# Moving the gate projection of a hybrid attention and recurrence block out of the projection stream

## The chip, the cores and the metric

The kernel runs on one core of one Trainium2 chip. The metric is the device time of one execution in microseconds, the median of several runs. The engines of the core are PE (matrix products, with weight loads as PEld), DVE, ACT and POOL (elementwise work), and SP, which only issues transfers. Each engine works through its own queue in order; transfers are issued from the queues of SP and ACT.

## The reference

Two layers run one after the other. Each takes 2048 latent tokens and 256 context tokens of width 1024 and computes

```
h    = rmsnorm(x) * (1 + scale) + shift            # per layer, from the conditioning vector
p    = h @ w_in + b_in                              # columns for four mixers, and 1024 gate columns
ya   = differential attention (4 heads, 2 maps each, all keys)
yb   = HGRN2, a gated linear recurrence in both directions
yc   = sliding-window attention (window 128) plus the context, with sinks
yd   = mLSTM in both directions, times a sigmoid of p's output-gate columns
x    = x + gate * ((concat(ya, yb, yc, yd) * silu(p_gate)) @ w_out)
```

Layer 1 (the last one) writes no context tokens, and a final rmsnorm follows it. Large products are made in three half-precision passes (high*high, high*low, low*high parts) that add up in one accumulator; the recurrences use f32 products.

## The kernel before

Tokens come in tiles of 128: 16 latent tiles and 2 of context. Layer 0 works on 18 tiles in every mixer, layer 1 on 16 in its outputs. Both layers run through the same stages, in this order.

**h.** Rows of x are normalised, transposed on PE (`hps`, L417), scaled (`ht`, L419) and split into `hh` and `hl` (L421, L422), which stay in SBUF for all projections. The first projections follow (`first_blocks`).

**Differential attention.** The loop at L1170 runs over units of one head and one tile: 72 in layer 0, 64 in layer 1. A unit has two maps; for each, `diff_scores` makes two halves of scores on PE (`scr`), DVE finds their minima (L1048), and `diff_exp` on ACT takes the exponential straight from PSUM. Each of the two halves has one PSUM buffer. Between these steps `pump(ns)` feeds PE from a filler, the generator `other_blocks`, until so much PE time has been issued: FSTEP between the two halves of scores, FGAP twice per unit after them. PE's order is the order written in this loop. The filler is the remaining projections. It walks two lists side by side, `heavy` (mLSTM values and keys, sliding-window keys and queries, both HGRN gates) and `light` (HGRN values, sliding-window values, output gate, two query blocks, and at its end four blocks of `gate_silu`).

**Rest.** What the filler has left runs in `rest_stream`, beside the first tiles of sliding attention (`swa_stream`) and mLSTM (`mlstm_stream`). `weave` picks, by positions in units of tiles and by waits in PE time, which stream issues next; RPOS is how much filler goes with one tile. `room(i)` lets both streams run only two tiles ahead of the output until the filler is done.

**Final.** When the filler is done, `hp` (h), the weights and the staging tiles are freed, and `hgrn_stream` and `out_stream` join sliding attention and mLSTM. Outside the attention loop the order of instructions on each engine is made by a scheduler that works from program order and its own estimates, so work from later in the program may be issued early if its memory is free.

`gate_silu` (L910) makes, per block of 256 gate columns and pair of tiles (a gate set), 48 products of 256 columns, then z (two DVE steps), a sigmoid (three ACT steps) and a product on POOL, and writes 256 KB to DRAM (`dgt`). `out_stream` reads `dgt` back as `gtt` (512 KB a tile). The four mixers write into one SBUF tile `yt` per token tile, of which six exist, and only attention's quarter goes through DRAM (`dy`). `out_stream` multiplies `yt` by `gtt` on POOL, transposes it on PE (`ft`), splits it, and makes 48 products of 512 columns (`fx`, one PSUM buffer) with `w_out`, whose two parts are prepared at its start from eight loads of 512 KB (`braw`, one buffer).

## Time and profile before

| | us |
|---|---|
| median of 3 runs | 4201.5 (4193.78 to 4209.3) |
| the profiled execution's own time | 4220.02 |
| span in its profile | 4218.2 |
| PE, DVE, ACT, POOL busy | 3570.4, 2873.5, 2332.9, 2358.5 |
| mean granted TensorE clock | 0.901 of full |

Busy times count instructions only; waits, and the issue of transfers, are not busy time. A granted clock of 1.00 is 2.4 GHz, 0.50 is 1.2 GHz, and a stretch between has some of both. Products on PE overlap in the record, so the time that a row of products takes is best read from the start of one to the start of the next.

### The profile page before, as it was taken

The page shows a single profiled execution, that of the slowest core. Times are in us where ns is not written, and L with a number is a line of the kernel's source. Part 1 is how long each engine was busy: PE and PEld are TensorE (multiplying, and loading weights), DVE is VectorE, ACT ScalarE, POOL GpSimd, SP SyncE. Part 2 cuts the span into 40 slices and gives each one's busy share as a digit, 9 for nine tenths or more (in the row PEclk, how much of TensorE's full clock was granted, in tenths as well). Part 3 has the DMA queues.
Part 4 walks back from the last instruction along what each step waited for, and adds up shares of the span by engine and source line. Part 5 has one row for each costly group of instructions (what it writes and reads, how often), then busy time and mean ns, then how long its engine had stood idle before and what let it go on. Part 6 is the DMA issues. An engine that isn't in the chain of part 4 may idle for free.

```text
span 4218.2 us, 78854 instructions
## 1 busy us (share of the span) xinstructions
PE 3570.4 (85%) x30342; PEld 2395.7 (57%) x30342; DVE 2873.5 (68%) x4550; ACT 2332.9 (55%) x4679; POOL 2358.5 (56%) x1727
## 2 busy tenths in 40 slices
PE   6988878888769987989998888788876798789998
PEld 3656655444547675556656476544444575556665
DVE  5168888888885546556643499888899766556664
ACT  5245656666655545555653366666666664555663
POOL 4443555443445458778857545645344554677883
PEclk7999989999989986888999999999998999778998
DMA  5356866667666547467754467566776662646662
GB/s 205 100 138 151 189 131 165 135 150 157 127 142 165 134 133 174 143 167 170 184 152 142 121 133 158 126 147 150 151 161 132 155 163 84 166 124 161 169 169 76
DMA packets 1256960, 622.19 MB, mean 148 GB/s; under 512 B 913476, under 2 KB 1203848, under 8 KB 1256584
## 3 DMA queue, kind: packets, MB, share of 16 engines
q1 hardware_dynamic: 1154216, 490.64, 51.2%
q10 hardware_dynamic: 102368, 126.52, 8.9%
q8 instruction: 239, 3.92, 0.4%
q14 instruction: 137, 1.12, 0.1%
HBM read 291.76 MB, written 131.23 MB: 100 GB/s over the span
## 4 chain that ended last, share of the span: by engine, by line
PE 31%; DVE 18%; POOL 8%; issue 7%; DMA 7%; ACT 5%; SPq 1%; ACTq 0%; POOLq 0%; DVEq 0%
PE fx L94 7%; PE ptm L94 5%; PE pfm L94 5%; DVE sm L1048 4%; PE go L94 4%; PE mnum L94 3%; PE scr L94 2%; ACT p L105 2%; DVE p L111 2%; POOL E L108 2%; DMA swt<-ph 1%; POOL yt L108 1%; PE gA L94 1%; PE ss L94 1%; DVE sm L108 1%
## 5 line engine op out<-in xcount | busy, mean ns | idle before, releaser
L108 POOL TENSOR_TENSOR p<-p,p 128x1024 f16<-128x1024 f32 (+2 forms) x264 | 623.4, 2362 | 793.7 <-ACT p L1084 704.4
L94 PE MATMUL ptm<-wb,hh 128*128 128x256 f16 (+2 forms) x5024 | 834.6, 273 | 30.3 <-DVE tm L111 7.4
L105 ACT ACTIVATE p<-scr,sm 128x1024 f32<-128x1024 f32 (+2 forms) x528 | 628.2, 1194 | 416.4 <-DVE sm L1073 143.3
L1048 DVE TENSOR_REDUCE sm<-scr 128x1 f32<-128x1024 f32 (+2 forms) x528 | 698.9, 1326 | 218.0 <-PE scr L94 214.2
L94 PE MATMUL pfm<-hh,wb 128*128 128x512 f16 (+1 forms) x2592 | 809.0, 376 | 26.5 <-DVE gz L111 10.4
L94 PE MATMUL ptm<-wb,hl 128*128 128x256 f16 (+2 forms) x2512 | 671.9, 273 | 1.8 <-POOL hl L108 1.8
L94 PEld LDWEIGHTS <-wb 128*128 128x128 f16 x3888 | 378.8, 101 | 410.8 <-issue 81.1
L94 PE MATMUL scr<-Ks,Qs 128*128 128x512 f16 (+1 forms) x1296 | 364.5, 380 | 289.2 <-ACT p L105 284.1
L94 PEld LDWEIGHTS <-hh 128*128 128x128 f16 x5024 | 479.0, 100 | 131.3 <-issue 37.7
L94 PE MATMUL pfm<-hl,wb 128*128 128x512 f16 (+1 forms) x1296 | 488.1, 377 | 0.0
L111 DVE SCALAR_TENSOR_TENSOR p<-p,sm,p 128x1024 f32<-128x1024 f32 (+2 forms) x264 | 414.6, 1571 | 8.2
L94 PE MATMUL fx<-wo,mh 128*128 128x512 f16 x1088 | 371.8, 426 | 6.2 <-DVE xt L111 2.7
L94 PEld LDWEIGHTS <-Qs 128*128 128x128 f16 x1296 | 130.4, 102 | 429.9 <-issue 359.5
L1084 ACT CAST p<-p 128x1024 f16<-128x1024 f32 (+2 forms) x264 | 297.4, 1126 | 40.0 <-DVE p L111 35.3
L94 PEld LDWEIGHTS <-wt 128*128 128x128 f16 x4640 | 245.1, 103 | 71.7 <-DMA wt<-p 23.6
L94 PE MATMUL pv<-Vs,wt 128*128 128x128 f16 (+1 forms) x4640 | 259.6, 214 | 22.1 <-DMA wt<-p 14.6
L94 PEld LDWEIGHTS <-hl 128*128 128x128 f16 x2512 | 250.6, 100 | 36.1 <-POOL hl L108 3.3
L94 PE MATMUL fx<-wo,mlo 128*128 128x512 f16 x544 | 230.0, 423 | 6.1 <-DVE mlo L108 5.9
L108 POOL TENSOR_TENSOR E<-lk,cm 128x512 f32<-128x512 f32 (+1 forms) x136 | 205.3, 1510 | 41.2 <-DMA cm<-dhc 19.7
L108 POOL TENSOR_TENSOR ph<-swp,ph 128x640 f16<-128x640 f32 (+2 forms) x136 | 190.7, 1402 | 59.5 <-ACT ph L1326 45.1
L108 DVE TENSOR_TENSOR QQ<-hq,E 128x512 f32<-128x512 f32 x119 | 148.1, 1253 | 73.6 <-ACT E L105 35.9
L105 ACT ACTIVATE E<-E 128x1024 f32<-128x1024 f32 x136 | 143.0, 1052 | 99.5 <-POOL E L108 93.1
(298 smaller groups left out, 6853.7 us busy)
## 6 DMA issues: line engine op xcount, KB each, us to landing
wraw<-in_w_in_dram SPq DMA_DIRECT2D x60, 512.0 KB
dgt<-ga ACTq DMA_DIRECT2D x68, 256.0 KB
r1b<-dr SPq DMA_DIRECT2D x68, 256.0 KB
gtt<-dgt SPq DMA_DIRECT2D x34, 512.0 KB
mraw<-in_w_mod_dram SPq DMA_DIRECT2D x64, 256.0 KB
vi<-dhi SPq DMA_DIRECT2D x49, 256.0 KB
KSb<-dsk SPq DMA_DIRECT2D x56, 192.0 KB
Ks<-dka SPq DMA_DIRECT2D x64, 144.0 KB
```

Of the source, the lines that this page charges most:

```text
L94: PE.matmul(o, lhsT=lhsT, rhs=rhs, start=start, stop=stop)
L105: A.activation(out=o, in_=i, func=f, **kw)
L108: return e.tensor_tensor(out=o, in0=a, in1=b, op=op)
L111: V.scalar_tensor_tensor(out=o, in0=a, scalar=s, in1=b, op0=op0, op1=op1)
L1048: V.tensor_reduce(sm[:, m * 2 + j:m * 2 + j + 1], ps[:, :n], AX.X, ALU.min)
L1084: A.copy(wl[:, :n], p[:, :n])
```

## The change

The gate projection leaves the filler. `h` is written to DRAM (`dh`, 256 KB for each part and tile, 36 writes a layer from ACT's queue), and `hh` and `hl` are laid out by tile. A new `gate_stream` reads h back tile by tile in the final stage, holds all 1024 gate columns of the weights in SBUF, and makes 48 products of 512 columns per tile; its result `ga` stays in SBUF for `out_stream`. Sliding attention and mLSTM are no longer held back by the output: they run with the rest of the filler (RPOS 12000) until all of the three are done, and only then the final stage begins, with gate, output and HGRN. All mixers' outputs go through `dy`; `out_stream` loads whole rows of it one tile ahead. FSTEP goes from 1100 to 600 ns in both layers, FGAP from 2500 and 2360 to 2300. Smaller edits: the HGRN prefix sums of two tiles in one scan, four small copies (`dn`) less per mLSTM tile, two buffers for `fx`, `gz`, `braw`.

```
-YTB, GPB, FXB, EB = 6, 4, 1, 3
+YTB, GPB, GLAG, EB = 3, 3, 1.0, 3
-    [... 32192.0, 1100.0, 2500.0],      # layer 0: ..., FSTEP, FGAP
-    [... 22000.0, 1100.0, 2360.0],      # layer 1
+    [... 32192.0, 600.0, 2300.0],
+    [... 22000.0, 600.0, 2300.0],
-    [38826.0, 42669.0, 12000.0, ...],   # layer 0: RPOS, SW0, HG0, ...
-    [40000.0, 23476.0, 6974.0, ...],    # layer 1
+    [12000.0, 12000.0, 12000.0, ...],
+    [12000.0, 12000.0, 6974.0, ...],
...
+                for t in range(n):
+                    for j, a in enumerate((hh, hl)):
+                        DQ.dma_start(dh[g0 // P + t, :, j], a[g][:, t])
...
-                    for i in range(nt):
-                        ...
-                        V.tensor_tensor_scan(out=o_, data0=ones_c, data1=f_, ...)
+                    for i in range(0, n, 2 * P):
+                        o_ = cu[:, i:i + 2 * P]
+                        o_ = o_[:, ::-1] if d else o_
+                        V.tensor_tensor_scan(out=o_, data0=ones_z.rearrange("p t q -> p (t q)"), data1=o_, ...)
...
-            ] + [((C_GATE + cb * 256, 256), lambda w, cb=cb: gate_silu(w, cb)) for cb in range(4)]
+            ]
...
-                    yield i, 0.0 if i else SW0, room(i)
+                    yield i, 0.0 if i else SW0, None
...
-                    o1 = yt_of(i)[:, 512:768].rearrange("p (h d) -> p h d", d=64)
+                    o1 = sw.tile([P, 4, 64], F32, tag="so1", name="so1")
...
+                    SP.dma_start(dy[qt * P:(qt + 1) * P, 512:768], o1)
...
-                            V.tensor_copy(dn[:, 1, d * 2:d * 2 + 2], TM[:, 2, d, js[d] * 4 + pa_:js[d] * 4 + 4:2])
...
+                    SP.dma_start(dy[order[i] * P:(order[i] + 1) * P, 768:], hqf)
...
+                    SP.dma_start(dy[cols, 256:512].rearrange("(t p) c -> p t c", p=P),
+                                 O.rearrange("p (t h) d -> p t (h d)", t=2))
...
+            def gate_stream():
+                wg = [fo.tile([P, KC, D], F16, tag=f"wg{j}", name=f"wg{j}", bufs=1) for j in range(2)]
+                bg = fo.tile([P, D], F32, tag="bg", name="bgt", bufs=1)
+                SP.dma_start(bg, b_in[l, C_GATE:C_GATE + D].partition_broadcast(P))
+                for b in range(8):
+                    s_ = slice(b * P, (b + 1) * P)
+                    raw = fo.tile([P, KC, P], F32, tag="braw", name="graw")
+                    SP.dma_start(raw, w_in[l][:, C_GATE + b * P:C_GATE + (b + 1) * P].rearrange("(k p) n -> p k n", p=P))
+                    act(wg[0][:, :, s_], raw, AF.Copy, scale=WS)
+                    stt(wg[1][:, :, s_], raw, WS, wg[0][:, :, s_], ALU.mult, ALU.subtract)
+                    yield 0.2 * b, 0.0, None
+                def load(i):
+                    ht = fo.tile([P, 2, KC, P], F16, tag="ht", name="htile")
+                    SP.dma_start(ht, dh[order[i]])
+                    return ht
+                nxt = load(0)
+                for i in range(len(order)):
+                    at = i + GLAG
+                    yield at, 0.0, lambda: i < done["out"] + YTB
+                    ht = nxt
+                    if i + 1 < len(order):
+                        nxt = load(i + 1)
+                    ga = gts[i] = fo.tile([P, D], F32, tag="ga", name="ga", bufs=YTB)
+                    for j in range(2):
+                        s_ = slice(j * 512, (j + 1) * 512)
+                        ps = gps.tile([P, 512], F32, tag="gz", name="gzp")
+                        for k in range(KC):
+                            mm(ps, ht[:, 0, k], wg[0][:, k, s_], k == 0, False)
+                            mm(ps, ht[:, 0, k], wg[1][:, k, s_], False, False)
+                            mm(ps, ht[:, 1, k], wg[0][:, k, s_], False, k == KC - 1)
+                            yield at + 0.5 * j + 0.06 * k, 0.0, None
+                        z = fo.tile([P, 512], F32, tag="gz", name="gz")
+                        stt(z, ps, IWS, bg[:, s_], ALU.mult, ALU.add)
+                        V.tensor_scalar(z, z, ZLOW, None, ALU.max)
+                        sigmoid(ga[:, s_], z)
+                        tt(G, ga[:, s_], ga[:, s_], z, ALU.mult)
+                    done["gate"] = i + 1
...
+                    need = min(i + 1, len(order) - 1)
+                    yield at, 0.0, lambda: done["hg"] > need and done["gate"] > i
+                    yt, xt = nxt or out_load(i)
+                    nxt = out_load(need) if need > i else None
+                    ga = gts.pop(i)
...
-            join(rest_stream(), swa_stream(), mlstm_stream())
-            weave(lambda: done["rest"])
+            join(rest_stream(), swa_stream(), mlstm_stream())
+            weave()
             wst.close()
             hst.close()
...
-            join(out_stream(), hgrn_stream())
+            st4.close()
+            gps = st5.enter_context(tc.tile_pool(name=f"gpt{l}", bufs=2, reuse_waits="tile", space=PSUM))
...
+            join(gate_stream(), out_stream(), hgrn_stream())
             weave()
```

## Rows read from the trace of the kernel before

**Rows 1.** Stages: length; busy PE, PEld, DVE, ACT, POOL; clock, DMA share, GB/s.
```profile
237.00:1290.00 1053.00, 849.39 (x7434) 563.73 (x7432) 866.94 (x1293) 615.28 (x1012) 479.91 (x277) 0.93 0.66 149
1290.00:1555.00 265.00, 247.34 (x1994) 183.80 (x1993) 136.94 (x301) 133.78 (x287) 123.93 (x114) 0.95 0.50 136
1555.00:2216.00 661.00, 594.62 (x5358) 395.96 (x5355) 378.81 (x674) 375.13 (x1010) 495.90 (x412) 0.82 0.65 167
2216.00:2385.00 169.00, 153.24 (x995) 99.96 (x993) 54.20 (x73) 58.08 (x97) 114.62 (x96) 0.97 0.44 137
2385.00:3300.00 915.00, 725.85 (x6375) 478.51 (x6373) 810.98 (x1133) 573.90 (x893) 445.14 (x244) 0.95 0.66 143
3300.00:3632.00 332.00, 281.28 (x2269) 205.03 (x2270) 199.89 (x368) 177.75 (x354) 162.93 (x135) 0.91 0.50 131
3632.00:4218.00 586.00, 522.52 (x4736) 348.32 (x4736) 349.68 (x596) 316.23 (x871) 421.57 (x350) 0.82 0.58 147
```

**Rows 2.** Waits of PE and of DVE in layer 1's attention: us, times, longest.
```profile
PE scr L94 <- ACT p L105: 157.2, 109, 6.9
DVE sm L1048 <- PE scr L94: 81.5, 119, 4.7
```

**Rows 3.** Busy time in parts of the final and rest stages, columns as in Rows 1.
```profile
1559.00:1648.00 89.00, 65.50 (x594) 54.08 (x594) 61.07 (x94) 51.67 (x137) 68.66 (x58) 0.54 0.80 198
...
1700.00:2216.00 516.00, 483.52 (x4342) 311.68 (x4342) 294.10 (x537) 293.20 (x805) 385.75 (x325) 0.88 0.63 165
...
3500.00:3632.00 132.00, 103.74 (x788) 71.39 (x786) 68.93 (x121) 60.07 (x98) 52.27 (x42) 0.90 0.27 88
```

**Rows 4.** PE in order of time: start, length, product, count.
```profile
2058.30 0.33 PE L94 MATMUL spv<-SVc,swt 128*128 128x128 f16 x4
...
2058.72 0.59 PE L94 MATMUL fx<-wo,mh 128*128 128x512 f16 x2
...
2059.37 0.59 PE L94 MATMUL fx<-wo,mh 128*128 128x512 f16 x2
...
2060.60 0.39 PE L94 MATMUL ss<-KSc,QS 128*128 128x256 f16 x2
...
2061.36 0.46 PE L94 MATMUL gA<-QQ,E 64*64 64x64 f32 x14
...
2063.46 0.44 PE L94 MATMUL mnum<-v,r1b 128*128 128x65 f32 x2
...
2064.19 0.43 PE L94 MATMUL mnum<-v,r1b 128*128 128x65 f32 x2
```

**Rows 5.** Tiles fx, mnum, gA, go and ss, each in 1700 to 2216, busy by engine.
```profile
1700.00:2216.00 516.00, 221.92 (x781) 22.44 (x33) 0.88 0.63 165
1700.00:2216.00 516.00, 78.16 (x416) 63.06 (x416) 10.95 (x26) 4.36 (x26) 0.88 0.63 165
1700.00:2216.00 516.00, 54.29 (x1792) 42.17 (x1792) 33.06 (x84) 14.81 (x42) 0.88 0.63 165
1700.00:2216.00 516.00, 66.01 (x336) 56.64 (x336) 5.20 (x14) 0.88 0.63 165
1700.00:2216.00 516.00, 37.04 (x327) 34.54 (x43) 37.53 (x86) 0.88 0.63 165
```

**Rows 6.** Groups of instructions in layer 0's rest stage: busy us, mean ns.
```profile
L94 PE MATMUL pfm<-hh,wb 128*128 128x512 f16 (+1 forms) x224 | 67.8, 375 | 2.7 <-DVE gz L111 2.0 <-ACT kT L722 0.7
...
L108 POOL TENSOR_TENSOR ga<-ga,gz 128x512 f32<-128x512 f32 x24 | 30.7, 1279 | 51.6 <-ACT ga L105 45.3 <-DMA vi<-dhi 3.4 <-DVE gz L111 2.6
```

**Rows 7.** Groups of the gate on DVE in layer 1's attention stage.
```profile
L916 DVE TENSOR_SCALAR gz<-gz 128x512 f32<-128x512 f32 x8 | 6.7, 832 | 0.0
L111 DVE SCALAR_TENSOR_TENSOR gz<-ptm,bg 128x512 f32<-128x512 f32 x8 | 5.4, 679 | 0.0
```

**Rows 8.** Issue of the gate's writes on ACT's queue: ns min/median/max.
```profile
L919 ACTq DMA_DIRECT2D dgt<-ga x68: 366/377/1507, 1078.3 to 3628.9; - x68
```

**Rows 9.** Page of the profile, part 3: transfers by packet size, whole span.
```profile
DMA packets 1256960, 622.19 MB, mean 148 GB/s; under 512 B 913476, under 2 KB 1203848, under 8 KB 1256584
```

More of the change, by code (lines that the diff above doesn't have):

```diff
@@ L139, in sigmoid @@
         act(o, o, AF.Exp, scale=-1.0)
-    ones_c = const.tile([P, P], F32, tag="ones", name="ones_c")
-    V.memset(ones_c, 1.0)
+    ones_z = const.tile([P, 2, P], BF16, tag="ones", name="ones_z")
+    V.memset(ones_z, 1.0)
+    V.memset(ones_z[:, :, 0:1], 0.0)
     ws_t = const.tile([P, 1], F32, tag="ws", name="ws_t")
@@ L290 @@
         dog = dt_("dog", [T, 256])
-        dgt = dt_("dgt", [T, D])
+        dh = dt_("dh", [NT, P, 2, KC, P], F16)
         dy = dt_("dy", [T, D])
@@ L1198 @@
                     u1, u2, u3 = u, u1, u2
-        with ExitStack() as st4:
+        with ExitStack() as st5:
+            st4 = ExitStack()
             sw = st4.enter_context(tc.tile_pool(name=f"sw{l}", bufs=2, reuse_waits="tile", side="right"))
@@ L1204 @@
             gps = st4.enter_context(tc.tile_pool(name=f"gps{l}", bufs=1, reuse_waits="tile", space=PSUM, side="right"))
-            gps2 = hg = fo = None
+            hg = fo = None
             order = all_tiles(cq)
             ngrp = len(order) // 2
-            done = dict(sw=0, ml=0, hg=0, out=0, rest=0)
-            yts = {}
-            turn_ = [0]
+            done = dict(hg=0, gate=0, out=0)
             def bank(shape, name):
-                turn_[0] += 1
-                if gps2 and turn_[0] % GPB == 0:
-                    return gps2.tile(shape, F32, tag="gp", name=name)
-                return gps.tile(shape, F32, tag="gp", name=name, bufs=GPB - 1)
-            def yt_of(i):
-                if i not in yts:
-                    yts[i] = (ml if i % YTB < 2 else fo).tile([P, D], F32, tag="yt", name="yt",
-                                                              bufs=2 if i % YTB < 2 else YTB - 2)
-                    t = order[i]
-                    SP.dma_start(yts[i][:, 0:256], dy[t * P:(t + 1) * P, 0:256])
-                return yts[i]
-            def room(i):
-                return lambda: i < done["out"] + (YTB if done["rest"] else 2)
+                return gps.tile(shape, F32, tag="gp", name=name, bufs=GPB if fo is None else GPB + 1)
             def states_of(src, g, n, pool, tag):
@@ L1391, in mlstm_stream @@
                 for i in range(len(order)):
-                    yield i, 0.0 if i else SW0, room(i)
+                    yield i, 0.0 if i else SW0, None
                     js, qt_, kt_, v1, r1b, g0b, og = nxt
@@ L1574, in out_stream, with out_load @@
+                    yield 0.2 * b + 1.0, 0.0, None
+                def out_load(i):
+                    r_ = slice(order[i] * P, (order[i] + 1) * P)
+                    yt = fo.tile([P, D], F32, tag="yt", name="yt", bufs=YTB)
+                    xt = fo.tile([P, D], F32, tag="xt", name="xt", bufs=YTB)
+                    SP.dma_start(yt, dy[r_])
+                    SP.dma_start(xt, x_rows(order[i], 1))
+                    return yt, xt
+                nxt = None
                 for i, t in enumerate(order):
@@ L1584, in out_stream @@
-                    tt(G, yt[:, 0:512], yt[:, 0:512], gt_[:, 0:512], ALU.mult)
-                    tt(G, yt[:, 512:], yt[:, 512:], gt_[:, 512:], ALU.mult)
+                    need = min(i + 1, len(order) - 1)
[3 more added lines that the diff above has]
+                    ga = gts.pop(i)
+                    for j in range(2):
+                        s_ = slice(j * 512, (j + 1) * 512)
+                        tt(G, yt[:, s_], yt[:, s_], ga[:, s_], ALU.mult)
@@ L1632, in join, with weave @@
                 live.extend([*next(g), pe_ns[0], g] for g in gens)
-            def weave(until=None):
-                while live and not (until and until()):
+            def weave():
+                while live:
                     may = [e for e in live if e[2] is None or e[2]()]
```

104 lines of the change are left out of this document (39 added, 65 removed).

## The prediction

> **What bounds the kernel now.** I read the busy times by stage first, then the waits of the attention stage, then PE in order of time to get the true pace of its products.
>
> The stages of [rows 1] have different limits. In attention DVE is busy for 867 of 1053 us (82%) in layer 0 and for 811 of 915 us (89%) in layer 1, PE for 81% and 79%. The waits there form a ring [rows 2]: PE's scores wait for ACT's exponentials to empty their one PSUM buffer (157 us in layer 1), and DVE's minima wait for the scores (82 us). Whatever PE does between two halves of scores lengthens the ring, and DVE's own work is a floor under it.
>
> In the rest stage PE is busy 93% and 85%. In the final stage it is busy 90% and 89%, at a granted clock of 0.82. That stage has a bad start: from 1559 to 1648 the clock is 0.54 while PE is busy 65.5 of 89 us [rows 3], because the output's weights are not ready and only small f32 products run. From 1700 on PE is busy 94% at 0.88, and nothing else is near full: POOL 386 of 516 us.
>
> **A unit of work.** The sum is made in PE work at full clock. Three `fx` products take 0.65 us from start to start, 0.217 each [rows 4]; an output tile is 48 of them, 10.4 us, plus eight f32 transposes that I put at half of 0.217 each (an estimate): 11.3. The gate's 48 products of 512 columns are also 10.4; a gate set of 48 at 256 columns is 5.2, so the total gate work is the same before and after. Four `mnum` records take 0.73 us [rows 4], 32 of them a tile 5.8, with 0.9 for the mLSTM scores (same estimate) 6.7. Sliding attention takes 0.76 for scores and 0.42 for values per head [rows 4], 4.7 a tile. HGRN's `gA` and `go` are busy 120 us for 14 tiles (1792 records, 128 a tile) at clock 0.88 [rows 5]: 7.6 a tile.
>
> How much of this fits into a microsecond? From 1700 to 2216 the counts of [rows 5] are 16.3 output tiles, 14 HGRN tiles, 13 mLSTM tiles and 43 heads: 184 + 106 + 87 + 51 = 428 us of work in 516 us, 0.83. In layer 0's rest stage 24 gate sets (125), 14 HGRN projection blocks of 24 products (224 records and half as many with `hl`, 73) [rows 6], some 20 for their states and some 33 for the first tiles (both estimates) make 251 in 265 us, 0.95. The dense f16 share of the work is 0.37 in the one and 0.87 in the other; between them I interpolate.
>
> **h, +5 us a layer.** 36 writes are added to ACT's queue; one issue takes 377 ns [rows 8], 13.6 us a layer, and none is on PE. A write of `hl` waits for POOL's last difference of its group, and the next group's `hh` copies queue behind it on ACT, for which POOL waits in turn. The bounds are nothing (ACT is idle most of that stretch: 58 of 169 us busy in layer 1) and 14; I take 5. The writes of `dgt` and its reads, equal in bytes, go. The added writes and reads of `dy` on SP's queue stand behind transfers that wait for POOL and PE, but `out_stream` asks a tile ahead; the cover is a tile's 30 us, and without it a round trip would show at each tile.
>
> **Attention.** PE gets less filler: per unit 2 x 500 + 2 x 200 = 1.4 us in layer 0 (72 units, 101 us) and 2 x 500 + 2 x 60 = 1.12 us in layer 1 (64 units, 72 us). If the ring sets the pace, all of that comes back. If DVE does, only its work counts that leaves: 12 gate sets in layer 0 (36 less the 24 of [rows 6]) and 8 in layer 1, at 1.5 us [rows 7], so 18 / 0.82 = 22 and 12 / 0.89 = 14 us. The heavy list gets a larger share of what remains, so the rest of DVE's work stays. Both limits are near here, so I take the middle: -61 and -43.
>
> **Rest, now with all of sliding attention and mLSTM.** Filler left over: in layer 0 93 us (the 73 and 20 above) plus 101 - 12 x 5.2 = 39, so 132; in layer 1 93 + 72 - 8 x 5.2 = 123. RPOS gives 12 us of it to each tile, so it lasts for 11 and 10.3 tiles. Up to there the work is 132 + 11 x 11.4 = 257 and 240, dense share 0.51, pace 0.86: 298 and 278 us. The remaining 7 and 5.7 tiles have only the two mixers, and PE is no longer the limit. Their price has bounds of 13.7 (11.4 / 0.83) and 22 us a tile. The latter is their transfers: in the rest stage the DMA share is 0.50 [rows 1], with filler alone 0.27 [rows 3], so 60 us in layer 0 and 76 in layer 1 belong to some 3.5 tiles, 17 and 22 each. I take 17, since little else moves then: 119 and 97. The stage takes 417 and 375 us against 265 and 332: **+152 and +43**. The `dn` copies that go save DVE time that PE covers.
>
> **Final.** A tile is 11.3 + 10.4 + 7.6 = 29.3 us of work, 527 and 469 in all. The dense share rises to 0.74, the pace to 0.92: 573 and 510. POOL loses more than it gets, so PE stays the limit. At the start sixteen weight loads instead of eight must land and be split, but gate products need only the first eight; loads for this stage can start in the tail of the one before, where memory of h is free. I put 20 us on the start: 593 and 530 against 661 and 586, **-68 and -56**. The bounds are the pace of 0.83 (655 and 585) and 0.95 with no loss at the start (555 and 494).
>
> **Sum.** Layer 0: 5 - 61 + 152 - 68 = +28. Layer 1: 5 - 43 + 43 - 56 = -51. Together -23 us on the profiled execution's 4220, which is 18 above the median shown; on the median 4201.5 this gives 4179. Less than 0.5% (21 us) can't be told from no change here, so this sits at that edge: work is moved between stages that are nearly all full, and the gain is what the bad start of the old final stage cost, less the new tail.
>
> **Rivals.**
> *The third stage runs on transfers.* At 19.5 us of transfers a tile (the middle of 17 and 22), 0.27 per us of filler, and 8.4 MB of early weights at the 198 GB/s and share 0.80 of [rows 3] (34 us), layer 0 needs 351 + 36 + 34 = 421 and layer 1 379 us of all sixteen engines. At a share of 0.9, more than any stretch of [rows 1, 3] has, that is 468 and 421 instead of 417 and 375: +97, 4276. It decides from 18 us a tile on. For it: mixers' transposes are packed into half the time. Against it: 17 was the dearer tile, with context, in layer 0. Chance 0.17. The Trainium skill (DMA: Bandwidth & Descriptors, Specifications) says that full rate wants transfers of at least 512 bytes; the trace has 913,476 of 1,256,960 packets below that [rows 9], and no stage above 0.66 of its engines, so it shows no saturation yet.
>
> *DVE holds attention.* Then attention gives 22 and 14, not 61 and 43, while the filler still lands in the next stage: +68, 4247. DVE's 89% in layer 1 speaks for it, its 82 us of waiting for scores against it. It decides when DVE's busy share passes 0.92. Chance 0.17.
>
> *The ring alone holds attention.* All 173 us come back instead of 104: 4110. Layer 0's DVE has 186 us idle, which would allow it; layer 1 has only 104. Chance 0.15.
>
> *The dense final stage keeps the clock.* At pace 0.95 and with no loss at its start it takes 555 and 494: -74, 4105. For it: the clock is 0.95 to 0.97 in the dense stretches of [rows 1]; against it: HGRN's f32 products remain. Chance 0.16. The Trainium skill (TensorE: Matmul & The Clock Gate, HAM oscillation) says that PE falls to half clock when its work has gaps, so gate products that are always at hand would hold it up; the trace agrees as far as 0.54 at the starved start goes [rows 3].
>
> **Chances and range.** My own case has 0.35, about 4140 to 4220. Faster by over 0.5%: 0.16 + 0.15 + 0.16 of my case; slower: 0.17 + 0.17 less a little that ends near zero, and some of my case. That makes 0.47 faster, 0.19 same, 0.34 slower. The range takes in the four rivals with their own spread: 4075 to 4285.
>
> **What would show it.** Attention near 992 and 872 us, with DVE's share up and the wait of scores for ACT down. Sliding attention and mLSTM over some 420 and 375 us, slow only after the last HGRN projection, DMA share near 0.8 or below. A final stage of about 590 and 530 us whose clock is above 0.88 and has no long stretch at 0.5. I am wrong if the tail of the third stage costs over 20 us a tile, if attention shortens by less than its DVE work, or if the final stage waits on `dy` or on weights.

## The result and the profile after

The changed kernel takes 4457.2 us (median of 4, 4457.0 to 4459.9); the kernel before, run beside it, 4205.4 us (median of 4). The ratio is 1.0603 with a 95% interval of 1.0577 to 1.0629: 6% slower, where 4179 us had been forecast.

The stages of the profiled execution of the changed kernel, columns as in [rows 1]. The mixer stage (sliding attention and mLSTM) is split where mLSTM ends, the final stage near where the output's products begin.

```profile
0.00:246.00 246.00, 197.61 (x1201) 123.92 (x1202) 77.24 (x117) 82.12 (x157) 115.28 (x101) 0.93 0.55 184
246.00:1240.00 994.00, 754.02 (x6569) 482.98 (x6568) 860.45 (x1252) 584.66 (x963) 463.42 (x263) 0.92 0.69 148
1240.00:1605.00 365.00, 345.29 (x2229) 238.58 (x2226) 206.70 (x445) 205.73 (x642) 225.48 (x245) 0.83 0.76 185
1605.00:1715.00 110.00, 65.69 (x504) 49.01 (x503) 40.28 (x98) 49.84 (x106) 49.94 (x41) 0.50 0.69 136
1715.00:1800.00 85.00, 59.71 (x489) 35.71 (x489) 42.15 (x46) 40.84 (x70) 39.38 (x28) 0.67 0.66 200
1800.00:2325.00 525.00, 510.89 (x4127) 281.94 (x4123) 199.59 (x300) 254.39 (x531) 319.56 (x219) 0.91 0.33 109
2325.00:2500.00 175.00, 153.13 (x957) 100.14 (x958) 53.87 (x80) 53.82 (x93) 107.35 (x92) 0.90 0.60 201
2500.00:3420.00 920.00, 687.03 (x5909) 442.33 (x5908) 829.02 (x1126) 558.37 (x872) 438.39 (x245) 0.92 0.64 137
3420.00:3795.00 375.00, 340.50 (x2154) 238.18 (x2152) 226.61 (x442) 221.38 (x630) 241.90 (x234) 0.76 0.76 176
3795.00:3890.00 95.00, 56.27 (x478) 39.44 (x477) 44.64 (x103) 48.79 (x103) 54.58 (x45) 0.66 0.72 155
3890.00:3995.00 105.00, 67.83 (x661) 41.40 (x662) 70.61 (x70) 48.85 (x83) 57.21 (x38) 0.67 0.54 164
3995.00:4458.00 463.00, 446.83 (x3453) 244.46 (x3451) 181.62 (x260) 197.09 (x434) 227.26 (x166) 0.91 0.27 91
```

These windows, and those of [rows 1], do not cut the stages at the same event. Attention's last products are `pv`, and they start last at 1275.2 and 3329.4 in the kernel before, at 1243.4 and 3447.8 in the changed one (kernel before first, layer 0 and then layer 1):

```profile
L94 PE MATMUL pv<-Vs,wt x2336: 190/220/314, 285.2 to 1275.2; 128*128 128x128 f16 x195
L94 PE MATMUL pv<-Vs,wt x2304: 190/219/314, 2425.7 to 3329.4; 128*128 128x128 f16 x192
...
L94 PE MATMUL pv<-Vs,wt x2336: 190/220/314, 289.7 to 1243.4; 128*128 128x128 f16 x195
L94 PE MATMUL pv<-Vs,wt x2304: 192/220/314, 2549.1 to 3447.8; 128*128 128x128 f16 x192
```

[rows 1] ends attention 15 us behind and 29 us ahead of them, the windows above 3 and 28 us ahead. So from here on, wherever a stage's length is compared between kernels, its ends are events of the trace: attention goes from the first `scr` product to the last `pv`, the rest or mixer stage from there to HGRN's first `gA` product, the final stage from there to the next layer's first `scr` or to the end. Layer 1's h stage overlaps layer 0's final stage and is counted with it. Lengths and changes in us, layer 0 / layer 1:

| stage | before | after | change | forecast change | miss |
|---|---|---|---|---|---|
| h of layer 0 | 238 | 246 | +8 | +5 | +3 |
| attention | 1038 / 947 | 997 / 942 | -40 / -5 | -61 / -43 | +21 / +38 |
| rest, then mixers | 279 / 312 | 472 / 447 | +192 / +136 | +152 / +43 | +40 / +93 |
| final, with layer 1's h | 828 / 577 | 791 / 563 | -37 / -14 | -63 / -56 | +26 / +42 |

The misses sum to 263 us, of which 133 are in the mixer stage. The reader is to see three things in the windows. While filler runs beside the mixers, PE is busy 95% and 91%, at a clock of 0.83 and 0.76. Then PE is busy 60%, DVE and ACT under half, at 0.50 in layer 0, near the lower of the clock's two levels: 29 heads of sliding attention (87 records of `swp` on ACT, three a head) run alone there. And the new final stage starts with 85 and 105 us at 0.67; its first output product (`fx`) comes 76 and 94 us after the first `gA`, where I had put 20 on the start.

The waits of that lone stretch of layer 0, 1605 to 1715 (us, times, longest):

```profile
ACT swp L105 <- DVE ssm L1296: 54.7, 28, 2.7
DVE ssm L1295 <- PE ss L94: 46.5, 28, 3.1
PE spv L94 <- DMA swt<-ph: 28.8, 25, 3.0
```

and ACT's exponentials in its timeline:

```profile
1639.58 0.79 ACT L105 ACTIVATE swp<-ss,ssm 128x640 f32<-128x640 f32 x1 [2.14 <-DVE ssm L1296]
...
1643.18 0.79 ACT L105 ACTIVATE swp<-ss,ssm 128x640 f32<-128x640 f32 x1 [1.96 <-DVE ssm L1296]
...
1646.78 0.79 ACT L105 ACTIVATE swp<-ss,ssm 128x640 f32<-128x640 f32 x1 [1.96 <-DVE ssm L1296]
```

One head every 3.60 us, each step waiting for the one before: PE's scores, DVE's maximum, ACT's exponential, and only then is the one score buffer `ss` free for the next head.

### The profile page after: what moved, and what is told of

It reads as the page before. It is cut to its first block, busy times and chain, and to the rows that moved or that the text cites. A ratio compares the mean times of both kernels' runs of the same rounds, so it can differ in the third digit from the quotient of the medians.

```text
span 4458.1 us, 75731 instructions
## 1 busy us (share of the span) xinstructions
PE 3684.8 (83%) x28710; PEld 2318.1 (52%) x28710; DVE 2832.8 (64%) x4335; ACT 2345.9 (53%) x4679; POOL 2339.7 (52%) x1710
## 5 line engine op out<-in xcount | busy, mean ns | idle before, releaser
L94 PE MATMUL pfm<-hh,wb 128*128 128x512 f16 (+1 forms) x2592 | 827.9, 382 | 40.3 <-ACT fm L105 18.7
L94 PE MATMUL ptm<-wb,hh 128*128 128x256 f16 (+2 forms) x2848 | 466.5, 271 | 12.8 <-DVE tm L111 10.8
L111 DVE SCALAR_TENSOR_TENSOR p<-p,sm,p 128x1024 f32<-128x1024 f32 (+2 forms) x264 | 442.8, 1678 | 8.2
L94 PE MATMUL gzp<-wg,htile 128*128 128x512 f16 x1632 | 432.0, 400 | 12.5 <-DVE gz L111 7.3
L94 PE MATMUL ptm<-wb,hl 128*128 128x256 f16 (+2 forms) x1424 | 373.4, 270 | 1.2 <-POOL hl L108 1.2
L94 PE MATMUL fx<-wo,mh 128*128 128x512 f16 x1088 | 330.9, 387 | 3.4 <-ACT mh L1618 3.4
L94 PEld LDWEIGHTS <-hh 128*128 128x128 f16 x2848 | 268.9, 101 | 83.4 <-issue 27.9
L94 PE MATMUL pv<-Vs,wt 128*128 128x128 f16 (+1 forms) x4640 | 270.6, 218 | 25.9 <-DMA wt<-p 21.2
L94 PEld LDWEIGHTS <-htile 128*128 128x128 f16 x1632 | 162.9, 102 | 206.3 <-issue 41.8
L94 PE MATMUL fx<-wo,mlo 128*128 128x512 f16 x544 | 208.0, 386 | 5.5 <-DVE mlo L108 5.5
```

The costliest lines, as they stand in the source:

```text
L94: PE.matmul(o, lhsT=lhsT, rhs=rhs, start=start, stop=stop)
L111: V.scalar_tensor_tensor(out=o, in0=a, scalar=s, in1=b, op0=op0, op1=op1)
```

## The experiments

Each run states its own ratio to the kernel before, which was run beside it each time (medians of 4204 to 4213 us).

### First four: the pump, the order, the score buffer, the weights

**Old pump.** `FSTEP` and `FGAP` back to 1100/2500 and 1100/2360.

> One edit to the changed kernel: the pump of filler into attention gets its two old numbers back in both layers (the step goes from 600 to 1100, the gap from 2300 to 2500 in layer 0 and 2360 in layer 1), all else stays. Theory (the short pump moves filler out of an attention stage that DVE holds into a mixer stage that PE holds): attention takes about 1050 us in layer 0 and 920 to 980 in layer 1 again (after: 994 and 920), the mixer stage loses more than that, 475 to about 375 in layer 0 and 470 to about 395 in layer 1; the sum is 20 to 120 us shorter, about 4340 to 4435. Rival one (the lone sliding attention sets the mixer stage's end whatever the filler): its 110 and 95 us stay, only the part before it shortens, and by what attention loses; 4440 to 4470. Rival two (the ring of scores holds attention in both layers): attention gains back 61 and 43 us of length and the sum is at 4457 or above.

Measured: 4565.5 us, ratio 1.0840 (1.0808 to 1.0871), against all three expectations. Attention takes 1063 and 1008 us, 66 more than in the changed kernel in either layer. The mixer stage has 429 and 306 projection products (`pfm`) less in it, 93 and 66 us at full clock (0.217 each), but takes 459 and 435, only 13 and 12 less. Filler is now done at 1380, and what follows shows why (windows, columns as in [rows 1]):

```profile
1290.00:1380.00 90.00, 76.83 (x435) 43.17 (x435) 39.20 (x83) 34.23 (x94) 44.90 (x46) 0.80 0.57 142
1380.00:1540.00 160.00, 127.72 (x762) 101.78 (x760) 69.99 (x170) 81.04 (x256) 85.95 (x89) 0.55 0.76 167
1540.00:1700.00 160.00, 141.58 (x737) 115.39 (x738) 73.52 (x167) 85.48 (x285) 97.28 (x107) 0.53 0.73 163
```

Both mixers together, without filler, get a clock of 0.55 and 0.53 although PE is busy 80% and 88%. From 1400 to 1700 the `mnum` products keep PE busy for 285 ns each (508 in 144.9 us), where it is 188 ns in [rows 5], and a tile of mLSTM with its sliding attention takes 18.9 us (508 records, 15.9 tiles). So the filler that the shorter pump leaves for this stage cost little there, 25 us for 159 us of products: it came with a higher clock.

**Sliding attention first.** Its planner positions are halved (`yield i + h / 6` becomes `yield 0.5 * (i + h / 6)`, and so on).

> One edit: the positions by which the planner of the mixer stage orders sliding attention are halved, so its heads are issued ahead of the filler and of mLSTM's tiles instead of behind them. Theory (sliding attention is a chain of 3.6 us a head through one score buffer in PSUM, and what is left of it when mLSTM has ended runs alone at a granted clock of 0.50): with its heads spread under the filler the lone 110 and 95 us mostly go, the mixer stages take 390 to 420 us each instead of 475 and 470, sum about 4310 to 4360. Rival one (transfers hold the stage): the stage is as long as before, with another order in it, 4440 to 4480. Rival two (PE's total work holds it): the lone part goes, but what is before it grows by the same PE time at full clock, so only about 50 us a layer are won less what mLSTM then waits: 4360 to 4430.

Measured: 4465.4 us, ratio 1.0602 (1.0571 to 1.0633), no change. From 1605 to 1715, where heads run alone, there are 84 records of `swp` on ACT instead of 87: the edit hardly moved a head and tells nothing of the theory.

**Two score buffers**, paid for with two of the three PSUM banks that mLSTM's products share (`GPB` is 3).

```
-  bufs=GPB if fo is None else GPB + 1        (mqk, mnum)
+  bufs=1 if fo is None else GPB + 1
-  ps = gps.tile([P, 1024], F32, tag="ss", name="ss")
+  ps = gps.tile([P, 1024], F32, tag="ss", name="ss", bufs=2)
```

> One edit: the score tile of sliding attention gets a second PSUM buffer, paid for with one of the two banks that mLSTM's products share (its qk products are then made a bank at a time). Theory (the chain through the one score buffer sets the pace of lone sliding attention): a lone head takes about 2.2 us instead of 3.6, the lone 110 and 95 us go to about 70 and 60, sum about 4380 to 4400, a little more if heads also get on faster beside mLSTM. Rival (transfers, or the transposes of p by DMA, set that pace): a lone head stays at 3.4 us or more and the sum within 20 us of 4457; above it if mLSTM misses its second bank.

Measured: 4391.9 us, ratio 1.0428 (1.0398 to 1.0458), 65 us less than the changed kernel, as the theory had it (4380 to 4400), but not by a faster lone head. Its mixer stage in four windows:

```profile
1235.00:1600.00 365.00, 335.05 (x2296) 231.95 (x2294) 201.44 (x446) 204.60 (x601) 218.18 (x225) 0.85 0.80 183
1600.00:1690.00 90.00, 75.01 (x434) 60.72 (x434) 34.92 (x91) 44.63 (x135) 48.27 (x53) 0.54 0.78 178
3415.00:3780.00 365.00, 332.30 (x2242) 232.04 (x2239) 215.28 (x457) 226.65 (x640) 239.75 (x237) 0.81 0.81 189
3780.00:3830.00 50.00, 41.69 (x317) 29.33 (x316) 32.19 (x74) 27.87 (x74) 33.69 (x32) 0.80 0.81 185
```

The stage takes 459 and 412 us instead of 472 and 447. Sliding attention keeps up with mLSTM, so no head is left to run alone; but in layer 0 mLSTM's last `mnum` now starts at 1700 instead of 1601, and from 1600 on both mixers share a clock of 0.54. The one buffer is worth 48 of the stage's 133 us of miss, 13 in layer 0 and 35 in layer 1.

**Weights early.** Gate and output weights get a pool of their own, opened when filler ends.

```
-            weave()
+            weave(lambda: done["rest"])
             wst.close()
             hst.close()
-            st4.close()
+            fw = st5.enter_context(tc.tile_pool(name=f"fw{l}", bufs=2, reuse_waits="tile"))
+            join(gate_weights(), out_weights())
+            weave()
+            st4.close()
```

> One edit: the weights of gate and output get a pool of their own, which is opened when the filler is done, so their loads and splits run beside the mixers' tail instead of after it. Theory (the final stage starts from nothing: in the changed kernel no load of it is issued before the last transposes of sliding attention, and 85 and 105 us go by before its first output products): the start shrinks to 20 to 35 us in each layer, sum about 4310 to 4350. Rival one (the transfers of the mixers' tail are slowed by the loads): the tail grows by 30 to 60 us a layer, the sum is 4380 to 4457. Rival two (the start is the round trip of h, gate and HGRN state, not the weights): the start stays at 60 us or more, 4400 to 4457.

Measured: 4464.8 us, ratio 1.0601 (1.0568 to 1.0634). Three windows, the end of the mixer stage and the start of the final stage in layer 0, then that start in layer 1:

```profile
1600.00:1745.00 145.00, 85.58 (x641) 66.98 (x642) 66.99 (x129) 69.47 (x148) 65.67 (x56) 0.50 0.77 167
1745.00:1815.00 70.00, 65.67 (x495) 34.84 (x490) 23.34 (x36) 30.87 (x62) 38.48 (x29) 0.89 0.35 115
...
3940.00:4005.00 65.00, 57.45 (x539) 32.66 (x540) 29.16 (x42) 31.43 (x63) 43.65 (x32) 0.86 0.31 105
```

The start is now work at 0.89 and 0.86, and the final stages are 29 and 31 us shorter than in the changed kernel (762 with layer 1's h, and 532). But the mixer stages take 504 and 487, 32 and 40 more: rival one's mechanism. What the start gave, the tail paid.

### Is PE or something else the limit of the mixer stage?

**Half the numerator** (the carried state's products left out; alone, then with two score buffers).

```
-  mm(num[:, d * 2 + pr], g0b[r_, d, pr], cst[r_, d, pr, i % 2], False, True)
```

> One edit to the changed kernel, which leaves part of the computation out: the products of the carried state (16 of the 32 f32 products that a tile's mLSTM numerator takes) are not made; all its transfers, PSUM tiles and other engines' work stay. Theory (PE holds the mixer stage, because f32 mixers run it at a low granted clock; 0.83 and 0.76 with filler beside them, 0.54 without): 16 products a tile at 0.42 us at half clock and some 0.23 at the others are 3.7 to 6.7 us a tile, 65 to 120 us in layer 0 and 60 to 105 in layer 1, of which some comes back as longer lone sliding attention: sum about 4300 to 4370. Rival one (transfers, or the chains of waits between engines, hold it): sum 4430 to 4457. Rival two (sliding attention's chain alone sets the end of the stage): mLSTM ends earlier and the lone part grows by as much, 4400 to 4457.

Measured: 4402.0 us, ratio 1.0447 (1.0416 to 1.0477), 55 less, between the theory and rival one. mLSTM ends no sooner (its last `mnum` starts at 1609, in the changed kernel at 1601), although PE has 16 products a tile less. PE's waits from 1300 to 1600 show what came next, the transposes of `p`; in the changed kernel PE waits for them 1.5 us and its weight loads 2.5 from 1240 to 1605:

```profile
PEld L94 <- DMA swt<-ph: 42.1, 21, 4.9
PE spv L94 <- DMA swt<-ph: 32.4, 17, 4.7
```

> Two edits to the changed kernel: two score buffers, and the mLSTM numerator without the products of the carried state (16 of 32 f32 products a tile left out, as before). It asks whether PE and sliding attention's chain hold the mixer stage together. Theory (both: whichever is relieved alone, the other ends last): against the run with two scores alone (4392, mixer stages 455 and 415) another 80 to 130 us go, stages about 400 and 360, sum 4265 to 4310. Rival (with two score buffers the stage runs on transfers, whose share is 0.80 there already): under 30 us go, 4360 or more.

Measured: 4339.9 us, ratio 1.0321 (1.0291 to 1.0351), 52 less than with two buffers alone; less than the theory's 80, more than the rival's 30.

**Without the loads of r1 and g0** (constant rows instead), with two score buffers, then with half the numerator too.

> Two edits to the changed kernel: two score buffers, and the rows r1 and g0 of each tile's mLSTM are not loaded (2 and 4 broadcast transfers a tile, 0.75 MB; one pair of tiles loaded once stands in for all, so the mLSTM's gates are left out; all engines' work stays). Theory (PE and the chains hold the stage): sum 4370 to 4395, DMA share of the mixer stage down from 0.80 to about 0.65. Rival (transfers hold it): a fifth of the bytes goes and so do 60 to 90 us of each mixer stage, sum 4230 to 4270.

Measured: 4371.7 us, ratio 1.0396 (1.0363 to 1.0429), 20 less than with two buffers alone.

> The three edits together (two score buffers, half of the numerator's products left out, r1 and g0 not loaded). If PE holds the stage with transfers close behind it, this falls well below each of the two runs that take away one: 4180 to 4250. If the chains of waits hold it, all three of these runs lie within 40 us of each other. If transfers alone hold it, this equals the run without the loads.

Measured: 4263.2 us, ratio 1.0138 (1.0093 to 1.0184), 129 less than with two buffers alone. The loads give 20 us while PE has all its work, 77 once it has half. By the mixer stage alone, both layers summed, it is 62 us for half the numerator (423 and 386), 41 for the loads (417 and 412) and 142 for both (371 and 357). So with two buffers PE's work comes first, transfers close behind it (share 0.78 to 0.81 above, 0.86 from 1520 to 1660 with half the numerator), and neither alone explains the stage.

### The clock

**Added products.** The changed kernel with the old pump, and after the last filler five products behind each mLSTM step.

```
+  ps = pps.tile([P, 512], F32, tag="pp", name="keep")
+  for k in range(5):
+      mm(ps.rearrange("p (t q) -> p t q", q=P), hh[0][:, 0, k], hh[0][:, 0, 0:4], k == 0, k == 4)
```

> The changed kernel with the old pump (4565; its mixers run without filler for 300 us of layer 0 and 240 of layer 1 at a clock of 0.54), and after the last filler five f16 products of 512 columns more behind each step of an mLSTM tile, whose result nobody reads; the program puts about 230 and 120 of them into the first half of the stretch without filler and none into the second. Theory (mixers alone lose the clock for want of dense products, and at half clock PE holds them): where the added products stand the clock is 0.75 or above, they cost little or nothing, mLSTM tiles get done in 17 to 20 us each there as without them, and the sum is 4540 to 4590. Rival (the clock is low for another reason): it stays at 0.54 to 0.6 and the products cost 0.43 us each, 100 and 50 us: sum 4680 or more. Rival (mixers are held by chains, and PE's clock does not matter): clock up, the same time per tile to within 5%.

Measured: 4557.0 us, ratio 1.0837 (1.0780 to 1.0894), the same as without the 350 added products (4547.2 and 4566.8 in its two executions, against 4565.4 and 4565.6). From 1400 to 1500, first the run with the old pump alone, all engines and then its `mnum`:

```profile
1400.00:1500.00 100.00, 78.19 (x482) 62.91 (x480) 43.25 (x105) 49.50 (x152) 53.31 (x55) 0.57 0.74 159
...
1400.00:1500.00 100.00, 34.14 (x130) 27.27 (x130) 3.36 (x8) 1.36 (x8) 0.57 0.74 159
```

and with added products: all engines, `mnum`, and the added ones:

```profile
1400.00:1500.00 100.00, 98.76 (x654) 65.94 (x655) 47.06 (x102) 51.34 (x179) 57.52 (x65) 0.90 0.78 173
...
1400.00:1500.00 100.00, 34.32 (x180) 27.94 (x180) 5.08 (x12) 2.03 (x12) 0.90 0.78 173
...
1400.00:1500.00 100.00, 45.05 (x168) 0.90 0.78 173
```

PE made 180 `mnum` products instead of 130 in the same 34 us of busy time, 191 ns instead of 263 each, and 168 products more on top. (Heads fell from 17 to 13, by the records of `swp`.) From 1600 to 1700, where no added product stands, the clock is 0.55 again. The clock is thus shown to depend on what PE is given beside the mixers, not on the stage. Two things aren't shown. One is which side of the edit raised it: the added products are of another kind, and they also filled PE's idle time (busy 78% without them, 99% with). The other is that the clock is what the stage's length hangs on: from the last filler to the last `mnum`, 512 `mnum` products and 47 heads took 319 us with added products and 317 without, so what the first 100 us won was lost in the next (153 `mnum` from 1500 to 1600 instead of 211), and the mixer stages took 457 and 435 us instead of 459 and 435.

**The same in the kernel before**, at the start of its final stage [rows 3], four and then eight products behind each step of mLSTM and HGRN.

> The kernel before with one addition: at the start of its final stage, where only small f32 products run (89 us at a clock of 0.54 in layer 0), four f16 products of 512 columns behind each step of mLSTM and HGRN until the first output tile, some 96 and 88 in the two layers, whose result nobody reads. Theory (f32 products alone lose the clock, dense ones beside them hold it, as in the run with added products): the clock of that stretch is 0.75 or more; the 65 us of PE time at 0.54 shrink to about 40 while the added ones take 21, so mixers get 10 to 25 us ahead in each layer: sum 4155 to 4190 against 4205. Rival (the stretch waits for the output's weights, and mixers that get ahead there wait later): within 10 us of before. Rival (the added products delay the mixers' own): 4215 or more.

> As the run before, with eight products behind each step instead of four (about 180 a layer, 39 us at full clock). Theory: the clock is no higher than with four and the added work is dearer: 5 to 25 us slower than with four. Rival (four are too few to hold the clock, eight do): faster than with four by 10 us or more.

Measured: 4224.7 us, ratio 1.0056 (1.0036 to 1.0075), and 4239.9 us, 1.0090 (1.0064 to 1.0115). With four:

```profile
1559.00:1648.00 89.00, 78.73 (x687) 52.60 (x687) 65.36 (x89) 51.67 (x126) 75.91 (x59) 0.73 0.68 186
```

The clock rose from 0.54 to 0.73, and the time rose too, by half a per cent: a higher clock alone bought nothing here. Why isn't shown. In the traces the first `fx` comes 17 us sooner after the first `gA` in layer 0 (75 against 92) and 9 us later in layer 1 (86 against 78), and layer 1's final stage loses 17 us of the 32 that layer 0's final stage with the next h gains. No version tried that makes the whole computation beats the kernel before.

### How much filler, and where

**A pump shorter still** (300 and 2000) with two score buffers; then with filler also spread out (`RPOS` 9000, the mixers' gaps 0); and the changed kernel's pump (600 and 2300) in the kernel before.

> Two edits to the changed kernel: the second score buffer of the run with two scores, and a pump shorter still (step 300 and gap 2000 instead of 600 and 2300, which moves 1.2 us of filler a unit, 86 and 77 us in all, out of attention). Theory (filler is dear in attention, 0.7 us of time for each us of PE in layer 0 and 1.2 in layer 1 by the run with the old pump, and nearly free in the mixer stage, where it lifts the clock from 0.54): attention 994 to about 935 and 920 to about 840, the mixer stages 430 to 480 us at a clock of 0.85 or more, sum 4230 to 4300. Rival (the mixer stage is at its end of PE time already, so moved filler lands there in full at a pace of 0.84): attention gains as much and the mixer stage grows by 100 and 90, sum about 4430 to 4460; if attention stands on DVE's own work, it gains nothing and the sum is above 4500.

> As the run before (second score buffer, step 300 and gap 2000), and the filler's position in the mixer stage rises by one for 9 us of PE work instead of 12, with the mixers' own gaps at nothing, so that filler lasts nearly to the end of the stage in layer 0 as well. Theory (mixers without filler beside them cost half the clock): no stretch of the mixer stage below a clock of 0.7; 10 to 40 us less than the run before. Rival (only the total of PE work counts): within 10 us of the run before. Rival (what filler does at the stage's start is to bridge chains of waits): some us longer than the run before.

> The kernel before with one edit: the pump's numbers of the changed kernel (step 600, gap 2300). It tells what the shorter pump is worth by itself. Theory (in the kernel before, filler holds gate products, which are light on DVE, so attention stands on the ring of scores there): attention 1053 to about 985 and 915 to about 850, the rest stage (PE busy 93% and 85%) grows by 100 and 70 us or a little more; sum 4210 to 4260. Rival (the moved filler is taken up by the idle time of the stage after): sum 4130 to 4190.

Measured: 4431.6 us, ratio 1.0517 (1.0486 to 1.0547), 40 more than two buffers with the pump as changed; 4505.8, 1.0693 (1.0645 to 1.0740); and 4291.8, 1.0185 (1.0155 to 1.0215). In the first, attention fell to 940 and 885 us, 57 and 47 less than with the pump as changed, but the mixer stages rose from 459 and 412 to 519 and 472, at 0.83 and 0.86: the rival's mechanism. In the second, filler outlasted the mixers, to 1712 against 1686 us in layer 0, and ran alone. In the kernel before, the shorter pump took 58 and 62 us off attention and put 118 and 115 on the rest stage. Of the three settings tried in a kernel with a mixer stage, the changed kernel's is the best: the old one costs 132 us of attention for 25 of mixers, the shortest costs the mixers 120 us for 104 of attention, and the final stages 24.

### Which part of the change costs

**Gate as filler again**, mixers still in their own stage, old pump.

```
+  ] + [((C_GATE + cb * 256, 256), lambda w, cb=cb: gate_silu(w, cb)) for cb in range(4)]
+  SP.dma_start(ga, dgt[r_])
-  join(gate_stream(), out_stream(), hgrn_stream())
+  join(out_stream(), hgrn_stream())
```

> The changed kernel with one of its two parts undone: the gate is projected again as filler from h in SBUF (24 of 36 and 24 of 32 sets or so of it in the mixer stage) and its rows come back from DRAM, with the pump's old numbers, which belong to it; h is not written out. Sliding attention and mLSTM keep their own stage, the final stage is output and HGRN alone. Theory (the mixer stage is dear for want of dense products beside f32 mixers, and attention lost its light filler when the gate left): attention takes 1053 and 915 us as before again (with the old pump and no gate in the filler it took 1044 and 1010); the mixer stage, now with some 125 us more of dense work, keeps a clock of 0.85 or more and takes 480 to 550 us in each layer; the final stage, 18 tiles less 10.4 us of gate at a pace of 0.88 and a start of 60 us, takes about 450 and 400. Sum 4200 to 4320, far under the 4565 of the old pump without the gate. Rival one (mixers in a stage of their own cost what they cost, whatever lies beside them: 475 us and the filler on top): mixer stage 600 or more, sum 4400 or more. Rival two (the gate's place does not matter, total PE work counts): 4450 to 4565.

Measured: 4460.6 us, ratio 1.0612 (1.0570 to 1.0655). That is not the theory's 4200 to 4320: attention took 1038 and 943 us, as in the kernel before and as it said, and the mixer stages 532 and 525, but the final stages 521 (to the last `fx`) and 489 instead of 450 and 400. The changed kernel is at 1.0603: the gate's move and the shorter pump together are worth nothing, and the loss is here without them. What is left of the change is the mixers' own stage, with the smaller edits that came with it (all outputs through `dy`, the scan of two tiles, the copies, the buffers); those were not tried one by one. Its mixer and final stages in layer 0:

```profile
1265.00:1690.00 425.00, 400.13 (x2881) 309.35 (x2882) 229.15 (x493) 237.95 (x715) 259.17 (x267) 0.81 0.75 173
1690.00:1800.00 110.00, 96.71 (x954) 76.43 (x951) 60.23 (x124) 59.52 (x117) 54.72 (x47) 0.95 0.66 148
1800.00:1865.00 65.00, 26.52 (x336) 21.91 (x336) 30.53 (x33) 30.14 (x53) 43.67 (x29) 0.50 0.67 204
1865.00:2335.00 470.00, 397.04 (x3425) 242.74 (x3424) 160.23 (x246) 196.22 (x439) 274.62 (x187) 0.79 0.40 133
```

The kernel before makes 15 of its 18 mLSTM tiles in layer 0 and 13 of 16 in layer 1 in its final stages, with their heads. Without them these stages are 147 and 88 us shorter (681 with layer 1's h, and 489, instead of 828 and 577), so beside output and HGRN they cost 235 us, 8.4 a tile. The stages that have them instead of the old rest stages are 253 and 213 us longer (532 and 525 instead of 279 and 312): 466, or 16.7 a tile. The difference of 231 us is the loss; the profiled execution is 227 longer than that of the kernel before. The gate, in turn, makes the final stage only 81 and 74 us longer (602 to the last `fx`, and 563, against 521 and 489) for 18 and 16 tiles of 10.4 us: there PE runs at 0.91 with it, at 0.79 without.

> The run before this and a second score buffer. Theory: where filler fills the whole stage the lone sliding attention is short, so the buffer gives less than the 65 us that it gave the changed kernel: 10 to 40 us less than without it. Rival (the chain through one buffer holds the stage even with filler): 60 us or more.

> The run before this (gate as filler, two score buffers) with the shorter pump of the changed kernel (step 600, gap 2300). Theory (filler is dear in attention only while it is the HGRN list; with gate in it the shorter pump gave 85 and 30 us there in the kernel before, and cost 130 and 93 in its PE-bound rest stage): 10 to 80 us more than with the old pump. Rival (a mixer stage with dense work beside it has room): less by 20 to 60 us.

Measured: 4433.1 us, ratio 1.0555 (1.0533 to 1.0577), 28 less, as the theory had it; and with the shorter pump 4480.4, 1.0660 (1.0638 to 1.0683), 47 more, as it had it too.

The counterpart, the gate per tile in a final stage that keeps the mixers, wasn't tried.

## Why the prediction was wrong

**The step that failed: "Rest, now with all of sliding attention and mLSTM".** It forecast +152 and +43 us and measured +192 and +136. The step lets the two mixers go on side by side, tile by tile, to the stage's end: 11 and 10.3 tiles beside filler at a pace of 0.86, the rest at 17 us a tile. They did not go so. By the step's own units the window from 1240 to 1605 holds 303 us of work (132 of filler, 18 mLSTM tiles, 43 heads), and the step's two rates give 367 us for it: in layer 0 that part was right. But all of mLSTM was done by then, and the 29 heads that were left, 34 us of work and 51 us by the step's rate, took 110. In layer 1 the window from 3420 to 3795 holds 280 us of work, 337 by the step's rates and 375 measured, at a clock of 0.76; the 22 heads left, 39 us by its rate, took 95.

Behind both lies a reading that failed: in the tail "PE is no longer the limit". With the old pump, both mixers without filler ran at a clock of 0.55 and 0.53 with PE busy 80 and 88%, and a tile took 18.9 us. The price of 17 us lay inside bounds of 13.7 and 22 that were taken from pace and from transfers; neither bound asks what clock the mix will get. (The dense share of 0.37 that the line of paces starts from is 0.40 by the counts beside it, 16.3 tiles of 10.4 in 428; that moves the paces by 0.01 at most.) The line of [rows 3] with 0.54 and PE busy 65.5 of 89 us was read as a bad start with weights missing. It holds mLSTM's and sliding attention's products, the mix that the change makes a stage of, and HGRN's beside them.

**One buffer of scores** stood in no step. In the kernel before, its chain of 3.6 us a head hides under output and HGRN; in a stage of two mixers it is last. The run with two buffers gives 65 us, 48 of them in the mixer stages.

**Attention** was forecast at -61 and -43 us and measured at -40 and -5. The term that failed is "The heavy list gets a larger share of what remains, so the rest of DVE's work stays". Four runs have layer 1's attention with and without the gate in the filler, at the old and the shorter pump. First with the gate (the kernel before, then with the shorter pump), then without it (old pump, then the changed kernel):

```profile
2382.80:3329.60 946.80, 745.13 (x6551) 490.44 (x6550) 834.94 (x1165) 589.19 (x916) 461.71 (x254) 0.94 0.66 142
2418.40:3303.60 885.20, 687.98 (x5944) 441.32 (x5943) 802.30 (x1019) 547.41 (x840) 424.21 (x225) 0.94 0.66 141
...
2557.50:3565.40 1007.90, 760.61 (x6480) 486.35 (x6479) 883.74 (x1236) 612.88 (x971) 498.65 (x284) 0.91 0.63 136
2506.00:3448.00 942.00, 700.47 (x6033) 451.03 (x6031) 851.66 (x1150) 571.81 (x891) 453.51 (x252) 0.91 0.64 137
```

The shorter pump takes 62 us off with the gate and 66 without it, most of the 72 of PE time that it moves: more than the middle that was taken. The gate's leaving puts 61 and 57 us on, with 49 us more of DVE's work at either pump, where the step had 12 us of it go. In layer 0 the pump is worth 58 and 66 us and the gate's leaving costs 26 and 18. The changed kernel with the gate back in its filler and the old pump (943 us, DVE 831) lies at the kernel before, so the smaller edits have no share in it.

**Final**: the pace was right or a little low (0.91 of clock, PE busy 97%). The start was not: 76 and 94 us to the first `fx` instead of 20. "Loads for this stage can start in the tail of the one before" did not hold as built, because no load of this stage's weights was issued before the tail's last transposes (the first at 1717.6, the last transpose at 1710.3); and where it was made to hold, the tail paid 32 and 40 us.

**h** was +8 instead of +5 in layer 0. In layer 1 it can't be told from the final stage: from layer 0's last `fx` to layer 1's first `scr` it is 189 us instead of 164, and in the kernel before layer 1's first transposes (`hps`) start 18 us ahead of that `fx`, in the changed one 14 us behind it.

**The rivals.** Transfers alone did not hold the stage: their share is 0.76, not 0.9, and with two buffers 16% of the stage's bytes less (69 and 65 MB instead of 82 and 77) gave 20 us. They stand close behind PE, as the run with both taken away shows. Attention in layer 1 gained less than the 14 us of the rival that DVE holds it, but not by that rival's mechanism: the pump's part came back nearly whole, as the ring alone would have it, and DVE got more work. The dense final stage did keep the clock (0.91), as the fourth rival had it, but not its start. Of the three signs of being wrong, the tail's was set at over 20 us a tile and did not show (29 heads alone in 110 us are 15 a tile); attention's, in layer 1, and the wait for weights did. The Trainium skill (TensorE: Matmul & The Clock Gate, HAM oscillation) puts the fall to half clock down to gaps in PE's work. The rows agree for the lone heads (PE busy 60%, clock 0.50). For both mixers they leave it open: PE was busy 80 to 88% at 0.53 to 0.55 there, and 84% at 0.79 in a final stage of output and HGRN (397 of 470 us from 1865, gate as filler), so PE's busy share alone does not tell the two apart; and the products that lifted the clock to 0.90 closed gaps as well as changed the mix.

What stays open is how the miss of some 85 us that is left in the mixer stage after two buffers divides between PE at its lower clock and transfers: taken away singly they give 52 and 20 us, together 129. That the lower clock is itself the cause is argued, not shown: where it was raised, the stage became no shorter.

## What to carry to other kernels

Price a moved piece of work by what it costs in the mix that it will have, the granted clock included: two mixers that cost 8 us a tile beside dense f16 work cost 17 in a stage of their own, part of it at half the clock. Ask of each chain through a single buffer what hides it now, and whether that goes along when the work is moved. Filler is not a sum to be moved at par: 159 us of products cost 132 in attention and 25 in the mixer stage, and some 160 more cost 120 there once it was full. And cut stages at the same event in both kernels before their lengths are compared: by the windows of [rows 1] and those shown here attention in layer 0 is 59 us shorter, by its last product 40.

## What the runs showed of the hardware

PE was busy 80 and 88% of two stretches and was granted a clock of 0.55 and 0.53: mLSTM's f32 products of 65 columns and sliding attention's f16 ones of 64 to 256 ran there, with the old pump. With 168 f16 products of 512 columns among them in 100 us it was 0.90, and an `mnum` product kept PE busy for 191 ns instead of 263. 350 products that nobody reads, 76 us at full clock, made that kernel neither slower nor faster (4557 against 4565 us).
